# Stores of kept operands on ScalarE's queue, decay gates in the k/b tile, and whole-kilobyte tiles at one address phase

## The chip, the cores and the metric

The kernel runs on one core of a Trainium2 chip. The metric is the device time of one execution in microseconds, the median of several runs; a profiled execution has a time of its own and a span from its first to its last instruction. The core's engines are TensorE (PE, with its weight loads PEld), VectorE (DVE), ScalarE (ACT), GpSimd (POOL) and SyncE (SP). SP computes nothing here: it issues DMAs from its queue, in order.

## The reference, cut to what matters

Two layers, each a mixer, a residual with LayerNorm, a gated feed-forward network and another residual with LayerNorm, over 1024 tokens of 1024 channels. The first mixer is RWKV-7, the second sparse attention (DSA) with an indexer and a top-256 gather.

```python
# layer 0: RWKV-7
xm = x[None] + xx[None] * mix[:, None, None, :]           # six mixed inputs
r, k, v = jnp.einsum('nbsd,nde->nbse', xm[:3], w_rkv)     # three projections
w_log = -jax.nn.softplus(-(w0 + jnp.tanh(xw @ w1) @ w2)) - 0.5
decay = jnp.exp(-jnp.exp(w_log))                          # decay gates
a = jax.nn.sigmoid(a0 + (xa @ a1) @ a2)
...                                                       # scan over tokens, head by head
return y @ w_o
# both layers
def conv_ffn(x, w_up, conv_w, conv_b, w_down):
    u = x @ w_up                                          # 1024 -> 5632
    u = sum(up[:, j:j + S] * conv_w[j] for j in range(CONV_W)) + conv_b
    gate, val = jnp.split(u, 2, axis=-1)
    return (jax.nn.silu(gate) * val) @ w_down             # 2816 -> 1024
```

## The kernel before, in words

**Products.** Nearly every product is made of three matmuls (`mm3`): each operand is split into a high part, rounded to fp32r, and a low part, which is what is left. ACT casts the high part (`split`, L54), POOL or DVE subtracts (L60). L65 is high by high, L66 and L67 have one low part each. A matmul streams the moving operand (512 columns, mostly) while the weights of the next are loaded.

**Stages.** RWKV takes 0 to about 1060 us, the first FFN runs to about 1830 (its up-projections 1130 to 1480, its down-projections after), DSA to about 2480, the second FFN to the end (up-projections 2590 to 2930).

**RWKV.** Tokens come in two halves (hf), channels in two groups (g): four units, (0,0), (0,1), (1,0), (1,1), at roughly 45 to 213, 213 to 460, 460 to 640 and from 640 us. In each unit `lora2` makes the decay gates (sigmoids, L483) and the gate a, `decays` scans the gates along tokens and takes exponentials (L496 to L508), and `proj` makes r, k and v (`pa` in PSUM), each from 8 steps kt of 12 matmuls. A step's operands are a pair of weight tiles (wh, wl) and a pair of mixed inputs (xmh, xml). `pair` (L402 to L416) makes them once and keeps them: they are stored to DRAM (L415, 192 stores of 256 KB), and the unit that needs them again loads them (L409): the inputs when g is 1, the weights when hf is 1. Weights (raw) come by L124. All of these DMAs are issued by SP. Operands, mixed inputs and the four gate tiles `sg` of a unit share the tag of `u`: 14 buffers of 2 KB per partition. `t` has 5 such buffers, AR 2 and BK 1 of 16 KB.

**FFN, up.** Strassen-like products: for each of 22 column blocks f, `up` runs seven products of 12 matmuls (L65 to L67, through `w_mm`). The moving tiles are x11, x21, x22 and the sums xT1 to xT4; the weights are `wo`, split by ACT and POOL from the loaded `wr` or from the sums that DVE makes (S, L884). Results are moved from PSUM (p, pS) into u by ACT (L995 to L1001) or added by DVE (L1004), then the convolution runs (`conv`, ACT L1010, DVE L1015) and the gate (L1023, L1024).

**What sets the order.** A scheduler places each engine's instructions from priorities and costs, and the engines then run their lists in order. Tiles get their addresses from pools that are opened and closed by stage; before the change a pool's tiles follow one another from wherever the pool starts.

Of the kernel before, what the change touches and what calls it, by code (L numbers as in the profile page):

```python
# [17 lines left out]
E05 = math.exp(-0.5)  # L18
# [6 lines left out]
V_MIX, V_W0, V_A0, V_KK, V_KA, V_RK = 0, 48, 56, 64, 72, 80  # L25
# [20 lines left out]
def f32(ap):  # L46
    return ap.bitcast(F32)
# [194 lines left out]
    yield  # L242


class Pools:


# [1 line left out]
        self.tc, self.open = tc, {}  # L249

    def add(self, name, **kw):
        cm = self.tc.tile_pool(name=name, bufs=1, reuse_waits="tile", **kw)
        pool = cm.__enter__()
        self.open[id(pool)] = cm
        return pool

    def psum(self, name, **kw):
        return self.add(name, space=bass.MemoryType.PSUM, **kw)

    def close(self, *pools):  # L260
        for p in pools:
            self.open.pop(id(p)).__exit__(None, None, None)


CFG = {'order': 'k0 r0 a0 A0 v0 x1 l0 l1 x0 d0 b0 i0 w0 W0 r1 d1', 'da': 'p', 'db': 'p', 'kk': 'p', 'uv': 'a', 'go': 'v', 'gz': 'p', 'wr': 'pppv', 'wk': 'vp', 'wv': 'pv', 'xl': 'ppp', 'xp': 'vppppppp', 'p1': 'q0 w q5 i4 t1 at i5', 'n1': 27, 'n2a': 26, 'n2b': 19, 'n3': 20, 'n4': 12, 'qp': 2, 'lag': 2, 'cm': 'pppp', 'phc': 'aaaa', 'olc': 'a', 'qm': 'av', 'quq': 'p', 'quk': 'v', 'sh': 16, 'tc': 'a', 'kve': 'a', 'cB': 'a', 'cU': 'a', 'cY': 'a', 'cV': 'aaaa', 'cR': 'aaaa', 'cT': 'a', 'cM': 'a', 'cUV': 'v', 'sq': 'a', 'kkE': 'a', 'pfl': 'n', 'l2': 'v', 'l1': 'v', 'wo0': 'vppvppvp', 'wl': 'ppvv', 'wl2': 'v', 'wl3': 'vv', 'gz2': 'v', 'yq': 'a', 'pfo': 0, 'pf0': 0, 'pf1': 1, 'pf2': 2, 'dwo0': 'pppppppp', 'dwl': 'vvvv', 'dwl2': 'v', 'dwl3': 'vv', 'tke': 'av', 'rt': 'f2 l0 z f0 f1 p0 p2 l1 f3 p1 p3 p4 l2 l4 l5 l3', 'dt': 'l0 a z l1 p0 p4 p2 p3 p1 l5 l2 l3 l4', 'eT1': 'pvpvvvpv', 'eT3': 'pvpvpppv', 'fs0': 'x0 x1 y1 y0 x2 y2 x3 y3 r0 r1 u0 r3 u3 r2 u4 u6 u2 u7 u5 u1', 'fs1': 'x0 y0 x1 x3 y1 x2 y2 r0 u0 y3 r1 r2 u1 r3 u3 u4 u2 u5 u6 u7', 'eT2': 'vvvvvvvv', 'e22': 'vvvvvvvv', 'eR': 'vvvvvvvv', 'tkp': 'vv', 'kvs': 1, 'ln0': 'pp', 'ln1': 'vv', 'ln2': 'pppppppv', 'ln3': 'pppppppv', 'ln4': ['pp', 'pp'], 'gl': 2, 'ga': '0g1g', 'dl0': 'pppppvppp'}
# [5 lines left out]
def rwkv(k, src, dst):  # L271
    nc, tc = k.nc, k.tc
    E = lambda n: nc.vector if CFG[n] == "v" else nc.gpsimd
    pools = Pools(tc)
    P_, M_ = pools.add("rw", side="left"), pools.add("rwm", side="left")
    PS = pools.psum("rwps")
    DR = k.dram
    zs = Rows(DR, "zs")
# [2 lines left out]
    def u(name, dt=F32):  # L281
        return P_.tile([128, 512], dt, name=name, tag="u", bufs=k.NU)

    def t(name, dt=F32):
        return M_.tile([128, 512], dt, name=name, tag="t", bufs=5)

    def w4(name, shape):
        return P_.tile(shape, F32, name=name, tag="w", bufs=1)

    def acc(name):  # L290
        return PS.tile([128, 512], F32, name=name, tag="acc", bufs=4)
# [18 lines left out]
    smask = M_.tile([128, 512], F32, name="smask")  # L310
# [91 lines left out]
    kept = {}  # L402

    def pair(key, make, again):

        if key in kept:
            hi, lo = u(key[0] + "h", F32R), u(key[0] + "l", F32R)
            for i, x in enumerate((hi, lo)):
                nc.sync.dma_start(f32(x), kept[key][i])  # L409
            return hi, lo  # L410
        hi, lo = make()
        if again:
            kept[key] = DR.tile([2, 128, 512], F32, name="kept_" + "_".join(map(str, key)))
            for i, x in enumerate((hi, lo)):
                nc.sync.dma_start(kept[key][i], f32(x))  # L415
        return hi, lo  # L416

    def operands(hf, n, g, kt):
# [11 lines left out]
    def prefetch(hf, n, g, m):  # L430

        for kt in range(m):
            ahead[hf, n, g, kt] = operands(hf, n, g, kt)
# [23 lines left out]
    def slot(ap, x):  # L457

        return ap.rearrange("p (c x i) -> p c x i", x=2, i=64)[:, :, x, :]

    def v2(ap):
        return ap.rearrange("p (c i) -> p c i", i=64)

    def lora2(hf, g):

        h_ = st[hf]
        AR = P_.tile([128, 4, 1024], F32, name="AR", tag="AR", bufs=2)
        s = un[hf, g] = dict(AR=AR, sg=[])
        if CFG["pfl"] == "b":
            prefetch(hf, 0, g, 1)  # L470
        w2 = wtile(k.w_w2[:, g * 512 : (g + 1) * 512], lo_eng=CFG["l2"])
        a2 = wtile(k.w_a2[:, g * 512 : (g + 1) * 512], lo_eng=CFG["l2"])
        if CFG["pfl"] == "a":
            prefetch(hf, 0, g, 1)
        for i in range(4):
            p = 4 * g + i
            sl = slice(i * 128, (i + 1) * 128)
            s["sg"].append(u("sg"))
            for o, w, h, v0 in ((v2(s["sg"][i]), w2, h_["hw"], V_W0), (slot(AR[:, i], 0), a2, h_["ha"], V_A0)):
                ps = acc("l2")  # L480
                nc.tensor.matmul(ps, w[0][:, sl], h, start=True, stop=False)
                nc.tensor.matmul(ps, w[1][:, sl], h, start=False, stop=True)
                s["last"] = nc.scalar.activation(o, v2(ps), AF.Sigmoid, bias=k.vec[:, v0 + p : v0 + p + 1])  # L483

    def decays(hf, g):
        s = un[hf, g]
        AR, sg = s["AR"], s["sg"]
        BK = P_.tile([128, 4, 1024], F32, name="BK", tag="BK", bufs=1)
        PC = M_.tile([128, 4, 8], F32, name="PC", tag="PC", bufs=2)
        s.update(BK=BK, PC=PC)  # L490
        with tc.issue_after(s["last"].ins):
            for i in range(4):
                p = 4 * g + i
                a_, r_, k_, b_ = slot(AR[:, i], 0), slot(AR[:, i], 1), slot(BK[:, i], 0), slot(BK[:, i], 1)
                c, ip = t("c"), t("ip")
                nc.vector.tensor_tensor_scan(c, smask, sg[i], 0.0, ALU.mult, ALU.add)  # L496
                nc.scalar.activation(ip, c, AF.Exp, scale=E05)
                nc.vector.tensor_tensor(sg[i], c, sg[i], ALU.subtract)
                E("db").tensor_tensor(b_, a_, v2(ip), ALU.mult)
                E("da").tensor_scalar(  # L500
                    a_, a_, k.vec[:, V_KA + p : V_KA + p + 1], omka[:, p : p + 1], ALU.mult, ALU.add
                )
                nc.vector.tensor_tensor(k_, a_, v2(ip), ALU.mult)
                nc.scalar.activation(c, c, AF.Exp, scale=-E05)
                nc.scalar.activation(a_, v2(sg[i]), AF.Exp, scale=-E05)
                nc.gpsimd.tensor_copy(PC[:, i, :], c[:, 63:512:64])
                nc.vector.tensor_tensor(r_, r_, v2(c), ALU.mult)

# [7 lines left out]
    def kproj(hf, g):  # L516
        s = un[hf, g]
        AR, BK = s["AR"], s["BK"]
        a = proj(hf, 1, g, False)
        prefetch(hf, 2, g, PF[2])  # L520
        ss = None
        for i in range(4):
# [4 lines left out]
            else:  # L527
                nc.vector.tensor_scalar(kk, a[i], k.vec[:, V_KK + p : V_KK + p + 1], None, ALU.mult)
            nc.vector.tensor_tensor(slot(BK[:, i], 0), slot(BK[:, i], 0), v2(a[i]), ALU.mult)
            sq = t("sq")  # L530
# [19 lines left out]
        for i in range(4):  # L550
            rb = mi("rb")
            nc.tensor.matmul(rb, selB[:, i, :], rnb, start=True, stop=True)
            nc.vector.tensor_tensor(slot(BK[:, i], 1), slot(BK[:, i], 1), v2(rb), ALU.mult)

# [277 lines left out]
    for j in range(-1, 5):  # L832
        for o in order:
            n, i = o[0], j + int(o[1:])
# [8 lines left out]
    first, last = finish0(Z0), finish1(Z1)  # L843
# [16 lines left out]
def ffn(k, layer, src, dst):  # L860
# [4 lines left out]
    nc, tc = k.nc, k.tc  # L865
    pools = Pools(tc)
    near, far = ("right", "left") if layer == 0 else ("left", "right")
    P_ = pools.add(f"ffp{layer}", side=near)
    L_ = N_ = None
    bufs = {"P": (3, 12), "L": (4, 0), "N": (0, 6)} if layer == 0 else {"P": (2, 12), "L": (5, 0), "N": (0, 7)}  # L870
    hd = [k.dram.tile([2, 128, T], F32, name=f"hd{layer}_{i}") for i in range(NF // 2)]
# [148 lines left out]
    def gated(f):  # L1020
# [4 lines left out]
        nc.sync.dma_start(hd[f // 2][f % 2], val)  # L1025

    psum, k.psum = k.psum, None
    xrs = {}
    w_load(0)
# [10 lines left out]
    for tt in range(4):  # L1040
        if psum:
            run(x_T(tt, lambda: psum("pt")))
        yield
    k.rows = None
    L_, N_ = pools.add(f"ffl{layer}", side=far), pools.add(f"ffn{layer}", side=far)
    PX, PY = pools.psum(f"ffpx{layer}", side="left"), pools.psum(f"ffpy{layer}", side="right")
    if not psum:
        for tt in range(4):
# [19 lines left out]
    half, more, rest = [], [4, 5, 6, 7], [0, 1, 2, 3]  # L1068
    first = [(f, n) for f in range(2) for n in ("11", "12")]
# [147 lines left out]
    for z in range(2):  # L1217
# [4 lines left out]
        i = B_LN + 4 * layer + 2 + z  # L1222
# [4 lines left out]
    for tt in range(8):  # L1227
# [11 lines left out]
        kw = {} if layer else dict(sums=sums, junk=L_.tile([128, 512], BF16, name="lnj", tag="lnj", bufs=1))  # L1239
# [6 lines left out]
def dsa(k, src, dst):  # L1246
    nc, tc = k.nc, k.tc
    TOPK = 256
    NEG = -1e30
    pools = Pools(tc)  # L1250
    P_, T_, PL = pools.add("dsp", side="right"), pools.add("dst", side="right"), pools.psum("dspl", side="right")
    zs = Rows(k.dram, "zd")

    def u(name, dt=F32):
        return P_.tile([128, 512], dt, name=name, tag="u", bufs=6)
# [37 lines left out]
    for h4 in range(2):  # L1293
        uk = u("uk")
        nc.sync.dma_start(uk, k.w_uk[:, 512 * h4 : 512 * h4 + 512])
        for g in range(2):
            gs = slice(64 * g, 64 * g + 64)
            for kt in range(2):
# [6 lines left out]
                o, lo = u("wqk"), u("wqkl", F32R)  # L1305
# [99 lines left out]
    for tt in range(8):  # L1405
# [1 line left out]
        if tt >= LAG:  # L1407
            early(2)
        yield
    M_, PS = pools.add("dsm", side="left"), pools.psum("dsps", side="left")  # L1410
    XTh = M_.tile([128, 4, 1024], F32R, name="XTh")
    XTl = M_.tile([128, 4, 1024], F32R, name="XTl")
    early(len(pend) - 2)
# [538 lines left out]
```

## Time and profile before

| | us |
|---|---|
| median of 3 runs | 3229.09 |
| lowest and highest | 3224.92, 3232.09 |
| profiled execution | 3245.21 |
| its span | 3243.4 |

Over the span PE is busy 2900.3 us (89%), DVE 2471.0 (76%), POOL 1530.5 (47%), ACT 1374.0 (42%). The mean granted clock of TensorE is 0.918 of full speed. A matmul's duration in a row is longer than its distance to the next, since matmuls are pipelined; pace is read from starts. An idle time is put down to the operation that ended it, and waits are given as the waiting engine and line, then who was waited for. SPq is SP's queue: a duration there is that of issuing a DMA, not of the transfer.

### The profile page before, as it was taken

What the parts mean: (1) busy time and instruction counts of PE and PEld (TensorE: products, weight loads), DVE (VectorE), ACT (ScalarE), POOL (GpSimd) and SP (SyncE); (2) the same over time, 40 slices, a digit from 0 to 9 for tenths busy, and PEclk for the clock granted to TensorE, in tenths of its full rate; (3) what the DMA queues carried; (4) which work ended last, traced back from release to release, by engine and by line L of the source; (5) the groups of instructions that cost most, each with busy time, mean ns of one, the idle gap of its engine ahead of it and who ended that gap; (6) DMA issues with size and microseconds to landing.
All of it is one profiled execution on the core that took longest, in us unless ns stands there. A gap on an engine that the chain in (4) does not pass through costs nothing. (4 is left out here: it accounts for less than half of the span.)

```text
span 3243.4 us, 41680 instructions
## 1 busy us (share of the span) xinstructions
PE 2900.3 (89%) x15032; PEld 2260.1 (70%) x15032; DVE 2471.0 (76%) x3925; ACT 1374.0 (42%) x2363; POOL 1530.5 (47%) x987
## 2 busy tenths in 40 slices
PE   7779889989898899999779888888998899999788
PEld 3568657767786677777667766656776677777577
DVE  6684767756757888888876789998475888888975
ACT  3532224322322444444223467776363544444331
POOL 2533105223135666667667612212313666666766
PEclk9878879879798899999889889999999999999899
DMA  5634533535316232235211511102214222235212
GB/s 180 246 131 166 178 101 129 171 118 175 115 56 205 81 89 78 78 91 201 85 65 55 200 56 57 55 33 95 76 48 160 68 78 78 79 98 201 78 52 91
DMA packets 236224, 356.44 MB, mean 110 GB/s; under 512 B 17290, under 2 KB 110858, under 8 KB 235634
## 3 DMA queue, kind: packets, MB, share of 16 engines
q1 hardware_dynamic: 236018, 353.79, 33.2%
q8 instruction: 118, 1.93, 0.2%
q14 instruction: 88, 0.72, 0.1%
HBM read 250.57 MB, written 103.15 MB: 109 GB/s over the span
## 5 line engine op out<-in xcount | busy, mean ns | idle before, releaser
L60 POOL TENSOR_TENSOR wo<-wr,wo 128x512 fp32r<-128x512 f32 x220 | 416.0, 1916 | 282.6 <-ACT wo L54 281.7
L1015 DVE SCALAR_TENSOR_TENSOR cv<-u,vec,cv 128x1023 f32<-128x1023 f32 (+1 forms) x176 | 347.7, 1993 | 53.0 <-ACT cv L1010 51.1
L65 PE MATMUL dn<-dh 128*128 128x512 f32 x532 | 220.8, 415 | 68.5 <-DVE acc L1142 68.3
L60 POOL TENSOR_TENSOR dl<-raw,dh 128x1024 fp32r<-128x1024 f32 x82 | 219.9, 2704 | 102.9 <-ACT dh L54 102.6
L65 PE MATMUL p<-xT,wo 128*128 128x512 f32 x528 | 214.4, 406 | 20.4 <-ACT u L999 11.4
L66 PE MATMUL dn<-dl,dh 128*128 128x512 f32 x532 | 218.2, 410 | 13.0 <-POOL dl L60 6.6
L67 PE MATMUL dn<-dh,dl 128*128 128x512 f32 x532 | 218.2, 410 | 0.0
L1010 ACT ACTIVATE cv<-u,vec 128x1024 f32<-128x1024 f32 x88 | 109.5, 1244 | 254.9 <-DVE u L1004 254.3
L1647 POOL TENSOR_TENSOR cm<-sc,toep 128x256 f32<-128x256 f32 x96 | 75.8, 796 | 293.4 <-DVE mn L1663 225.0
L66 PE MATMUL p<-xT,wo 128*128 128x512 f32 x528 | 210.1, 398 | 3.0 <-DVE xT L60 3.0
L67 PE MATMUL p<-xT,wo 128*128 128x512 f32 x528 | 209.8, 397 | 2.0 <-POOL wo L60 2.0
L1142 DVE SCALAR_TENSOR_TENSOR acc<-acc,dn 128x512 f32<-128x512 f32 x196 | 130.9, 680 | 88.1 <-PE dn L67 88.0
L60 POOL TENSOR_TENSOR wo<-S,wo 128x512 fp32r<-128x512 f32 x88 | 172.7, 1981 | 30.7 <-ACT wo L54 26.4
L54 ACT CAST dh<-raw 128x1024 fp32r<-128x1024 f32 x95 | 94.7, 1046 | 201.2 <-PE dn L67 89.0
L60 POOL TENSOR_TENSOR wl<-wr,wh 128x512 fp32r<-128x512 f32 x56 | 74.8, 1336 | 214.7 <-ACT wh L54 158.1
L65 PEld LDWEIGHTS dn<-dh 128*128 128x128 f32 x532 | 105.7, 199 | 99.1 <-DVE acc L1142 42.0
L65 PE MATMUL pa<-xmh,wh 128*128 128x512 f32 x256 | 114.8, 458 | 48.8 <-ACT xmh L54 24.5
L65 PEld LDWEIGHTS p<-xT,wo 128*128 128x128 f32 x528 | 99.9, 189 | 60.6 <-ACT u L999 27.3
L65 PE MATMUL p<-x,wo 128*128 128x512 f32 x352 | 139.3, 396 | 0.8 <-DVE t L884 0.4
L54 ACT CAST wo<-wr 128x512 fp32r<-128x512 f32 x220 | 127.2, 618 | 28.0 <-POOL wo L60 18.9
L66 PE MATMUL p<-x,wo 128*128 128x512 f32 x352 | 138.7, 394 | 0.0
L67 PE MATMUL p<-x,wo 128*128 128x512 f32 x352 | 138.5, 394 | 0.0
(422 smaller groups left out, 8682.5 us busy)
## 6 DMA issues: line engine op xcount, KB each, us to landing
wr<-in_w_up_dram SPq DMA_DIRECT2D x88, 512.0 KB, 5.9
hd<-cv SPq DMA_DIRECT2D x44, 512.0 KB, 3.4
raw<-hd SPq DMA_DIRECT2D x19, 1024.0 KB, 5.0
raw<-in_w_down_dram SPq DMA_DIRECT2D x19, 1024.0 KB, 7.8
wr<-in_w_wo_dram SPq DMA_DIRECT2D x68, 256.0 KB, 2.9
wr<-in_w_rkv_dram SPq DMA_DIRECT2D x48, 256.0 KB, 3.6
kept_w<-wh SPq DMA_DIRECT2D x48, 256.0 KB, 2.3
kept_w<-wl SPq DMA_DIRECT2D x48, 256.0 KB, 2.1
```

The costliest lines, as they stand in the source:

```text
L54: nc.scalar.copy(hi, raw)
L60: eng.tensor_tensor(lo, raw, f32(hi), ALU.subtract)
L65: mm(ps, lhs[0], rhs[0], start=start, stop=False, **kw)
L66: mm(ps, lhs[0], rhs[1], start=False, stop=False, **kw)
L67: mm(ps, lhs[1], rhs[0], start=False, stop=stop, **kw)
L1010: nc.scalar.activation(o, u, AF.Identity, bias=k.vec[:, cb : cb + 1], scale=k.vec[:, cw[2] : cw[2] + 1])
L1015: nc.vector.scalar_tensor_tensor(o[:, d:], u[:, : 1024 - d], k.vec[:, cw[j] : cw[j] + 1], o[:, d:], ALU.mult, ALU.add)
L1142: nc.vector.scalar_tensor_tensor(o, o, ALPHA if first else 1.0, ps, ALU.mult, ALU.add)
L1647: (nc.vector if CFG["cm"][h4] == "v" else nc.gpsimd).tensor_tensor(cm[:, :near], mk, toep[g][:, h % 8, 256 - near :], ALU.add)
```

## The change

Three parts.

1. `pair` issues the stores of kept operands from ACT (`nc.scalar.dma_start`) rather than from SP. 192 issues leave SP's list (875 rows become 686) and enter ACT's (1560 become 1774).
2. The decay gates are written into the first half of each channel block of BK, the tile that later holds k and b, rather than into four `u` tiles. BK is therefore allocated in `lora2`; in `decays` the difference of scan and gate goes to a new `t` tile d, where it was written in place. k and b then overwrite the gates.
3. `Pools.add` returns an `Even`: two pools, one for tiles whose bytes per partition are a multiple of 1024, one for all others, padded at its end so that the first kind stands at the same address modulo 1024 (992) in every stage.

The cut diff (a line of "..." where something is left out):

```diff
+PHASE = 1024
+SKEW = 576
+class Even:
+    def __init__(self, tc, name, first=False, **kw):
+        self.parts, self.first, self.odd = [], first, {}
+        for n in ("odd", ""):
+            cm = tc.tile_pool(name=name + n, bufs=1, reuse_waits="tile", **kw)
+            self.parts.append((cm, cm.__enter__()))
+    def tile(self, shape, dtype, name, tag=None, bufs=1):
...
+        if n % PHASE == 0 and tag not in self.odd:
+            return self.parts[1][1].tile(shape, dtype, **kw)
+        key = tag or name
+        self.odd[key] = max(self.odd.get(key, 0), -(-n // 32) * 32 * bufs)
+        return self.parts[0][1].tile(shape, dtype, **kw)
+    def close(self):
+        rest = (SKEW * self.first - sum(self.odd.values())) % PHASE
+        if rest:
+            self.parts[0][1].tile([128, rest // 4], F32, name="rest")
...
     def add(self, name, **kw):
-        cm = self.tc.tile_pool(name=name, bufs=1, reuse_waits="tile", **kw)
+        return Even(self.tc, name, **kw)
...
-                nc.sync.dma_start(kept[key][i], f32(x))
+                nc.scalar.dma_start(kept[key][i], f32(x))
...
         AR = P_.tile([128, 4, 1024], F32, name="AR", tag="AR", bufs=2)
-        s = un[hf, g] = dict(AR=AR, sg=[])
+        BK = P_.tile([128, 4, 1024], F32, name="BK", tag="BK", bufs=1)
+        s = un[hf, g] = dict(AR=AR, BK=BK)
...
-            s["sg"].append(u("sg"))
-            for o, w, h, v0 in ((v2(s["sg"][i]), w2, h_["hw"], V_W0), (slot(AR[:, i], 0), a2, h_["ha"], V_A0)):
+            for o, w, h, v0 in ((v2(BK[:, i, :512]), w2, h_["hw"], V_W0), (slot(AR[:, i], 0), a2, h_["ha"], V_A0)):
...
-                c, ip = t("c"), t("ip")
-                nc.vector.tensor_tensor_scan(c, smask, sg[i], 0.0, ALU.mult, ALU.add)
+                c, ip, d = t("c"), t("ip"), t("d")
+                nc.vector.tensor_tensor_scan(c, smask, BK[:, i, :512], 0.0, ALU.mult, ALU.add)
+                nc.vector.tensor_tensor(d, c, BK[:, i, :512], ALU.subtract)
                 nc.scalar.activation(ip, c, AF.Exp, scale=E05)
-                nc.vector.tensor_tensor(sg[i], c, sg[i], ALU.subtract)
...
-                nc.scalar.activation(a_, v2(sg[i]), AF.Exp, scale=-E05)
+                nc.scalar.activation(a_, v2(d), AF.Exp, scale=-E05)
```

`first` is set for the first pool of a side of the memory in each stage, and PSUM's pools stay as they were.

Addresses in bytes per partition, modulo 256, of the tiles that move and of the weights, before. Afterwards all of them stand at 224.

| products | moving tiles | weight tiles |
|---|---|---|
| first FFN, up | x11, x21, xT4: 224; xT1, xT2, xT3, x22: 160 | wo: 224 |
| second FFN, up | x11, x21: 160; xT1 to xT4, x22: 32 | wo: 160 |
| DSA, logits | Q: 224 | XTh, XTl: 160 |

The order of the instructions in DSA and both FFNs is the same on every engine but for the first few of the first FFN.

ACT, the first projection of the first unit (steps kt 0 and 1), before:

```order
L54 CAST wh<-wr 128x512
L351 ACTIVATE xm<-xT,omm 128x512
L54 CAST xmh<-xm 128x512
L351 ACTIVATE xm<-xT,omm 128x512
L54 CAST wh<-wr 128x512
```

And with the change:

```order
L54 CAST wh<-wr 128x512
L387 ACTIVATE xm<-xT,omm 128x512
L451 DMA kept_w_0_0_389<-wh 128x512
L451 DMA kept_w_0_0_389<-wl 128x512
L54 CAST xmh<-xm 128x512
L387 ACTIVATE xm<-xT,omm 128x512
L451 DMA kept_xm_0_0_399<-xmh 128x512
L451 DMA kept_xm_0_0_399<-xml 128x512
L54 CAST wh<-wr 128x512
```

Each cast of a high half now has two stores ahead of it, and the second of them needs the low half of the cast before (wl, xml), which POOL or DVE makes.

SP, the same place, steps kt 2 and 3, before (kept_w_0_2 is the weight of step 2 of projection 0):

```order
L415 DMA kept_xm_0_2_458<-xmh 128x512
L415 DMA kept_xm_0_2_458<-xml 128x512
L124 DMA wr<-in_w_rkv_dram 128x512 x3
L415 DMA kept_w_0_3_479<-wh 128x512
L415 DMA kept_w_0_3_479<-wl 128x512
```

And with the change, from the end of the gate's stores:

```order
L432 DMA gsc<-tg_330 32x512
L124 DMA wr<-in_w_rkv_dram 128x512 x22
L124 DMA wr<-in_w_w_dram 128x512
L124 DMA wr<-in_w_a_dram 128x512
L124 DMA wr<-in_w_rkv_dram 128x512 x3
L445 DMA xmh<-kept_xm_0_0_399 128x512
L445 DMA xml<-kept_xm_0_0_399 128x512
```

The loads of raw weights no longer alternate with stores: 22 stand in a row, and the loads of kept inputs follow without a store between.

## Rows read from the trace of the kernel before

**Rows 1.** Busy us by stretch; last columns: granted clock, DMA share, GB/s.

```profile
45.00:213.00 168.00, 124.71 (x562) 95.41 (x562) 120.05 (x150) 85.18 (x144) 84.28 (x64) 0.83 0.58 206
...
1130.00:1480.00 350.00, 343.35 (x1469) 273.85 (x1468) 302.40 (x215) 160.87 (x244) 240.72 (x124) 1.00 0.30 82
```

**Rows 2.** Timeline of PE in an up-projection: start us, duration us, instruction.

```profile
1239.64 0.39 PE L66 MATMUL p<-x,wo 128*128 128x512 f32 x1
...
1241.91 0.39 PE L67 MATMUL p<-x,wo 128*128 128x512 f32 x1
1242.13 0.39 PE L65 MATMUL p<-xT,wo 128*128 128x512 f32 x1
...
1247.50 0.40 PE L67 MATMUL pS<-xT,wo 128*128 128x512 f32 x1
```

**Rows 3.** Instructions of L66, moving tile x, 1130 to 1470: ns min/median/max.

```profile
L66 PE MATMUL p<-x,wo x136: 389/389/390, 1137.1 to 1461.2; 128*128 128x512 f32 x136
...
L66 PE MATMUL pS<-x,wo x68: 393/394/398, 1131.6 to 1453.0; 128*128 128x512 f32 x68
```

**Rows 4.** Timeline of DVE over one block f, idle time in brackets.

```profile
1234.15 0.69 DVE L1004 TENSOR_TENSOR u<-u,pS 128x512 f32<-128x512 f32 x1 [1.44 <-PE pS L67]
...
1244.66 1.78 DVE L884 TENSOR_TENSOR S<-S,wr 128x512 f32<-128x512 f32 x1
...
1254.11 0.69 DVE L1004 TENSOR_TENSOR u<-u,pS 128x512 f32<-128x512 f32 x1 [1.42 <-PE pS L67]
```

**Rows 5.** Timeline of ACT and PE in the same block.

```profile
1246.53 1.14 ACT L54 CAST wo<-S 128x512 fp32r<-128x512 f32 x2 [3.73 <-DVE S L884]
1247.58 0.58 ACT L999 COPY u<-p 128x512 f32<-128x512 f32 x1
...
1248.21 0.50 PE L65 MATMUL p<-xT,wo 128*128 128x512 f32 x1 [0.31 <-ACT u L999]
```

**Rows 6.** Waits of PE, 1130 to 1480: us, times, longest us.

```profile
PE p L65 <- ACT u L999: 5.6, 17, 0.7
```

**Rows 7.** Waits of PE, 1480 to 1830 (first FFN, down).

```profile
PE dn L65 <- DVE acc L1142: 37.3, 8, 13.2
```

**Rows 8.** Groups on PE, 1830 to 2480 (DSA): busy us, mean ns, idle.

```profile
L65 PE MATMUL lg<-XTh,Q 128*128 128x512 f32 x96 | 43.2, 450 | 9.7 <-DVE mn L1663 7.2 <-DVE Q L60 1.0 <-DVE v L1542 0.9
```

**Rows 9.** Waits of SP's queue, 0 to 700: us, times, longest us.

```profile
SPq L415 <- POOL xml L60: 39.0, 38, 3.5
...
SPq L415 <- POOL wl L60: 33.7, 26, 5.4
...
SPq L409 <- ACT AR L505: 16.5, 4, 12.2
```

**Rows 10.** Instructions by line: issues of L415; low halves on POOL, 45 to 213.

```profile
L415 SPq DMA_DIRECT2D kept_w<-wh x48: 319/327/445, 51.0 to 382.0; - x48
...
L60 POOL TENSOR_TENSOR wl<-wr,wh x16: 1262/1290/1859, 51.1 to 209.2; 128x512 fp32r<-128x512 f32 x16
...
L60 POOL TENSOR_TENSOR xml<-xm,xmh x21: 1267/1548/1742, 54.7 to 179.2; 128x512 fp32r<-128x512 f32 x21
```

**Rows 11.** Waits of ACT, 45 to 213: us, times, longest us.

```profile
ACT B L604 <- PE bps L603: 22.2, 8, 4.5
ACT wh L54 <- DMA wr<-in_w_rkv_dram: 12.7, 3, 7.2
```

**Rows 12.** Timeline of SP's queue around the start of unit (0,1).

```profile
210.63 0.32 SPq L415 DMA_DIRECT2D kept_w<-wl  x1
211.04 0.39 SPq L409 DMA_DIRECT2D xmh<-kept_xm  x1
```

**Rows 13.** Timeline of SP's queue in unit (1,1).

```profile
656.13 0.32 SPq L409 DMA_DIRECT2D xmh<-kept_xm  x1
```

**Rows 14.** Timeline of PE at both places, idle time in brackets.

```profile
213.73 0.77 PE L65 MATMUL pa<-xmh,wh 128*128 128x512 f32 x1 [6.33 <-DMA xmh<-kept_xm]
...
658.70 0.77 PE L65 MATMUL pa<-xmh,wh 128*128 128x512 f32 x1 [9.59 <-DMA xmh<-kept_xm]
```

More of the change, by code (lines that the diff above doesn't have):

```diff
@@ L242, in once @@
     yield
+PHASE = 1024
[7 more added lines that the diff above has]
+    def tile(self, shape, dtype, name, tag=None, bufs=1):
+        n = mybir.dt.size(dtype)
+        for x in shape[1:]:
+            n *= x
+        kw = dict(name=name, tag=tag, bufs=bufs) if tag else dict(name=name)
+        if n % PHASE == 0 and tag not in self.odd:
[7 more added lines that the diff above has]
+            self.parts[0][1].tile([128, rest // 4], F32, name="rest")
+        for cm, _ in reversed(self.parts):
+            cm.__exit__(None, None, None)
 class Pools:
@@ L251, in add, with psum @@
     def add(self, name, **kw):
-        cm = self.tc.tile_pool(name=name, bufs=1, reuse_waits="tile", **kw)
+        return Even(self.tc, name, **kw)
+    def psum(self, name, **kw):
+        cm = self.tc.tile_pool(name=name, bufs=1, reuse_waits="tile", space=bass.MemoryType.PSUM, **kw)
         pool = cm.__enter__()
@@ L255, in add @@
         return pool
-    def psum(self, name, **kw):
-        return self.add(name, space=bass.MemoryType.PSUM, **kw)
     def close(self, *pools):
         for p in pools:
-            self.open.pop(id(p)).__exit__(None, None, None)
+            if isinstance(p, Even):
+                p.close()
+            else:
+                self.open.pop(id(p)).__exit__(None, None, None)
 CFG = {'order': 'k0 r0 a0 A0 v0 x1 l0 l1 x0 d0 b0 i0 w0 W0 r1 d1', 'da': 'p', 'db': 'p', 'kk': 'p', 'uv': 'a', 'go': 'v', 'gz': 'p', 'wr': 'pppv', 'wk': 'vp', 'wv': 'pv', 'xl': 'ppp', 'xp': 'vppppppp', 'p1': 'q0 w q5 i4 t1 at i5', 'n1': 27, 'n2a': 26, 'n2b': 19, 'n3': 20, 'n4': 12, 'qp': 2, 'lag': 2, 'cm': 'pppp', 'phc': 'aaaa', 'olc': 'a', 'qm': 'av', 'quq': 'p', 'quk': 'v', 'sh': 16, 'tc': 'a', 'kve': 'a', 'cB': 'a', 'cU': 'a', 'cY': 'a', 'cV': 'aaaa', 'cR': 'aaaa', 'cT': 'a', 'cM': 'a', 'cUV': 'v', 'sq': 'a', 'kkE': 'a', 'pfl': 'n', 'l2': 'v', 'l1': 'v', 'wo0': 'vppvppvp', 'wl': 'ppvv', 'wl2': 'v', 'wl3': 'vv', 'gz2': 'v', 'yq': 'a', 'pfo': 0, 'pf0': 0, 'pf1': 1, 'pf2': 2, 'dwo0': 'pppppppp', 'dwl': 'vvvv', 'dwl2': 'v', 'dwl3': 'vv', 'tke': 'av', 'rt': 'f2 l0 z f0 f1 p0 p2 l1 f3 p1 p3 p4 l2 l4 l5 l3', 'dt': 'l0 a z l1 p0 p4 p2 p3 p1 l5 l2 l3 l4', 'eT1': 'pvpvvvpv', 'eT3': 'pvpvpppv', 'fs0': 'x0 x1 y1 y0 x2 y2 x3 y3 r0 r1 u0 r3 u3 r2 u4 u6 u2 u7 u5 u1', 'fs1': 'x0 y0 x1 x3 y1 x2 y2 r0 u0 y3 r1 r2 u1 r3 u3 u4 u2 u5 u6 u7', 'eT2': 'vvvvvvvv', 'e22': 'vvvvvvvv', 'eR': 'vvvvvvvv', 'tkp': 'vv', 'kvs': 1, 'ln0': 'pp', 'ln1': 'vv', 'ln2': 'pppppppv', 'ln3': 'pppppppv', 'ln4': ['pp', 'pp'], 'gl': 2, 'ga': '0g1g', 'dl0': 'pppppvppp'}
@@ L274, in rwkv @@
     pools = Pools(tc)
-    P_, M_ = pools.add("rw", side="left"), pools.add("rwm", side="left")
+    P_, M_ = pools.add("rw", first=True, side="left"), pools.add("rwm", side="left")
     PS = pools.psum("rwps")
@@ L486, in decays @@
         s = un[hf, g]
-        AR, sg = s["AR"], s["sg"]
-        BK = P_.tile([128, 4, 1024], F32, name="BK", tag="BK", bufs=1)
+        AR, BK = s["AR"], s["BK"]
         PC = M_.tile([128, 4, 8], F32, name="PC", tag="PC", bufs=2)
-        s.update(BK=BK, PC=PC)
+        s.update(PC=PC)
         with tc.issue_after(s["last"].ins):
@@ L867, in ffn @@
     near, far = ("right", "left") if layer == 0 else ("left", "right")
-    P_ = pools.add(f"ffp{layer}", side=near)
+    P_ = pools.add(f"ffp{layer}", first=layer == 1, side=near)
     L_ = N_ = None
@@ L1044, in ffn @@
     k.rows = None
-    L_, N_ = pools.add(f"ffl{layer}", side=far), pools.add(f"ffn{layer}", side=far)
+    L_, N_ = pools.add(f"ffl{layer}", first=layer == 0, side=far), pools.add(f"ffn{layer}", side=far)
     PX, PY = pools.psum(f"ffpx{layer}", side="left"), pools.psum(f"ffpy{layer}", side="right")
@@ L1409, in dsa @@
         yield
-    M_, PS = pools.add("dsm", side="left"), pools.psum("dsps", side="left")
+    M_, PS = pools.add("dsm", first=True, side="left"), pools.psum("dsps", side="left")
     XTh = M_.tile([128, 4, 1024], F32R, name="XTh")
```

## The prediction

> **What bounds the kernel now.** I read the busy time per stretch first, then the PE timeline of an up-projection, then what PE waits for, and last SP's and ACT's queues in the RWKV layer. In the first FFN's up-projections PE is busy 343.35 of 350 us at a granted clock of 1.00; in the first RWKV projections (45 to 213 us) it is busy 124.71 of 168 us, with ACT busy 85.18 us [rows 1]. So a faster matmul has its best chance in the FFN, and a change of queues only in the RWKV layer.
>
> The pace of matmuls shows what the alignment can touch. In [rows 2] the ten steps from 1239.64 to 1241.91 take 2.27 us, 0.227 us each; the 23 steps from 1242.13 to 1247.50 take 5.37 us, 0.2335 us each. Instruction, shape and clock are the same. What differs is the moving tile: x11/x21, whose address modulo 256 equals that of the weight tiles, against xT and x22, which stand elsewhere (the table of addresses in the section on the change). By tile, p<-x lasts 389 ns at its median, and pS<-x (x22) 394 ns [rows 3]. I read it as 6.5 ns lost where the moving operand and the weights loaded meanwhile have different phases. By the addresses some 4,100 of 9,200 wide matmuls are such before, and about 100 after.
>
> But PE being busy is not PE setting the pace. PE waits 17 times in this stretch for ACT u L999, 5.6 us in all [rows 6]: once per column block f of about 19.95 us. Followed back, that wait is a loop through three engines. DVE waits 1.44 us for PE's pS and starts at 1234.15 [rows 4]; after that neither it nor ACT waits for PE again until S L884 (start 1244.66, 1.78 us). ACT casts S (1246.53) and only then empties the bank (u L999 at 1247.58, 0.58 us) [rows 5]; PE resumes at 1248.21 and reaches the next pS, for which DVE waits 1.42 us until 1254.11 [rows 4]. Of the 19.96 us from 1234.15 to 1254.11, 14.06 us are DVE and ACT work and 5.9 us PE's. **Only the matmuls in those 5.9 us shorten the loop**; the rest turn into a longer wait for u L999.
>
> **Part 3, alignment: the terms.** The 5.9 us hold 24 matmuls, all xT or x22, all of unequal phase: 24 x 6.5 ns = 0.156 us per block. Times 22 blocks and two FFNs (the second has the same order, and its xT and x22 are out of phase too): **-6.8 us**. If PE alone set the pace it would be 48 matmuls per block in the first FFN and 60 in the second, 108 x 22 x 6.5 ns = 15.4 us; that is the other end. In the down-projections some 280 matmuls change phase, 1.8 us, but PE there waits 37.3 us for DVE acc L1142 [rows 7], so I take **-1**. In DSA the logits, scores and absorbed queries hold some 720 wide matmuls and 384 of half width, at most 6 us; the lg matmuls wait 7.2 us for DVE mn L1663 [rows 8], a loop over other engines again, so I take a third, **-2** (0 to -6). In RWKV some 200, mostly at half clock or beside waits: **-0.5**. Nothing in the change shortens DVE, ACT or POOL work. Sum: -10.3 us, between -4 and -23.
>
> The Trainium skill speaks against all of this: "SBUF — State Buffer", section "SBUF: two separate sides", says that on the engine side only the port pair shared by VectorE and GpSimd causes contention, that PE never waits on anyone, and lists a second independent read port for the weight load. By it the alignment is worth nothing, which is rival B. The trace differs as far as it goes: 389 against 394 ns.
>
> **Part 1, stores from ACT.** Removed: 192 issues on SP, which stood in order before the loads. SP's waits for POOL's low halves are 39.0 us (xml) and 33.7 us (wl) [rows 9]: time in which no load behind them goes out. Where PE paid is visible at 213.73: PE sat 6.33 us for xmh from DRAM [rows 14]; SP had the load behind the store of wl, which went at 210.63, and issued it at 211.04 [rows 12]. With the store elsewhere the load can go about 6 us earlier, but this step's wl comes only at 210.6, so PE gains about 3 us, not 6.33. The load one step earlier stands behind such a store in the same way; another 3. ACT waits 12.7 us for weight loads that SP sent late, the longest 7.2 us [rows 11]; in the new order SP sends 22 in a row; PE's part of that I put at a quarter, 3. Gain: **-9**, between 0 and -16.
>
> Added: the same 192 issues on ACT, in order between its casts. The trace of before has no issue on ACT; SP's takes 319 to 445 ns [rows 10], so between 0 and 0.45 us each; I take 0.32, near its median of 327 ns. Worse than the issue is the wait: ACT now stands until the low half exists before it casts the next high half. From 45 to 213 us there are 24 steps and 96 stores. ACT's 85.2 us grow by 96 x 0.32 = 31 to 116. POOL's low halves take 1.29 us (wl) and 1.55 us (xml) [rows 10]; 24 x 2.84 = 68 us, less some 15 for the xm copies that stand between cast and store: 53. That makes 169 of 168 us, before ACT's other waits, such as 22.2 us for PE bps [rows 11]. So **ACT goes from half idle to just full** there. Lower bound 0 (all falls into its 83 idle us), upper bound 169 + 22.2 + 12.7 - 168 = +36. I take a third, **+12**, since PE's own sum in the stretch leaves 43 us and low halves already made PE wait. In the two later units only w or only xm is stored, one wait and two stores per step, and ACT is far from full: **+2** (0 to +8). Queued behind the waits on ACT are the next casts (then POOL, then PE), the evictions of the projections and the copies of the chunk recurrence.
>
> **Part 2, gates in BK.** The four sg tiles no longer take 4 of the 14 u buffers. At 658.70 PE had waited 9.59 us for xmh [rows 14], whose load SP issued only at 656.13 [rows 13], after waiting up to 12.2 us for ACT AR L505 [rows 9], the last reader of sg. That wait has no cause any more. Next late is the decay chain itself, which still ends at the same place on ACT; I take two thirds, **-6** (0 to -10). Allocating BK earlier makes the sigmoids wait for the previous unit's last reader of BK, which in the trace is done before they start: 0. The extra t tile per pass takes 3 of 5 buffers: 0 to +2.
>
> **Sum.** -10.3 - 9 + 12 + 2 - 6 = -11.3 us. The profiled execution took 3245.21 us, 0.5% above the median of the three timed runs (3229.09); I take the difference as absolute: 3234 for such an execution, **3218** for the median.
>
> **Rivals.** A: PE alone sets the pace of the up-projections, so all 15.4 us count. For it: PE's 343.35 of 350 us; against it: the wait for u L999 in nearly every block. 8.6 us more: 3209. B: alignment gives nothing and 389 against 394 ns comes from something else, such as where the moving tiles lie; only RWKV is left, -1: 3228. C, slower: ACT becomes the bound of the first unit and stays late into the second. It decides as soon as waits and issues exceed ACT's 83 idle us, and my sum is 84. At the price of +36 +8 instead of +14 the total is +19: 3248; half of the excess gives 3233. For it: the strict order cast, store, store on ACT; against it: PE already waits there for other things, and freed u buffers let ACT run ahead. D: ACT absorbs the issues and all stalls go (-16, -10): -36 + 2 = -34: 3195. For it: PE's idle time in 45 to 213 us; against it: low halves come when POOL makes them. That the change is not what it says is excluded for order and addresses, which the built kernel shows.
>
> **How the numbers follow.** Forecast 0.44, A 0.12, B 0.10, C 0.16, D 0.18. About 0.2% (6.5 us) is what a measurement of this kernel can tell from no change, so faster means under 3222.6, slower over 3235.5. Faster: 0.33 of the forecast (its own spread is 3206 to 3232), all of D, most of A: 0.62. Same: the rest of the forecast, most of B, the mild end of C: 0.21. Slower: most of C and a little of the forecast and of B: 0.17. The range 3192 to 3234 leaves out the bad half of C and the far end of D.
>
> **What would show it.** Alignment: p<-xT and pS at 389 ns; the up-projection block at 19.8 us, not 19.5 (A) nor 19.95 (B); PE's wait for u L999 above 0.4 us per block. Stores: ACT's waits for POOL wl and xml in 45 to 213 us near 50 us, and that stretch longer by some 10 us; no stall at 213. Gates: no wait of L409's loads for AR, and PE's 9.59 us gone. Wrong I am above all if ACT's issue costs far from 0.32 us, or if PE in the first unit follows ACT step by step.

## The result: slower by 0.9%, and the profile after

The changed kernel took 3262.78 us (median of 4), before 3230.08: a ratio of 1.0093, 95% interval [1.0072, 1.0113]. The two medians alone divide to 1.0101, inside the interval. Measured again later the ratio was 1.0096 [1.0064, 1.0129]. I had forecast 3218 with a range to 3234.

The profiled execution of the changed kernel took 3262.46 us, 17 us more than that of before (3245.21). The latter lies 8 to 15 us above the medians measured for its kernel, so the two traces understate the difference; all verdicts below go by the timed runs, and the traces say where.

**The first unit.** Busy us of PE, PEld, DVE, ACT and POOL from the first projection matmul of unit (0,0) to the first of unit (0,1); then the granted clock. Before, the changed kernel:

```profile
52.20:201.80 149.60, 115.35 (x536) 89.35 (x537) 106.93 (x135) 73.01 (x122) 74.21 (x56) 0.83 0.62 221
```

```profile
53.90:216.50 162.60, 124.61 (x536) 90.66 (x537) 89.89 (x122) 72.10 (x119) 66.00 (x53) 0.83 0.60 209
```

The same 536 matmuls take 13.0 us longer. What ACT does there, from its timeline (start us, duration us; ACTq rows are issues of DMAs):

```profile
62.17 0.62 ACT L54 CAST xmh<-xm 128x512 fp32r<-128x512 f32 x1 [1.19 <-POOL wl L60]
62.69 0.72 ACT L387 ACTIVATE xm<-xT,omm 128x512 f32<-128x512 f32 x1
62.82 0.33 ACTq L451 DMA_DIRECT2D kept_xm<-xmh  x1
64.18 0.33 ACTq L451 DMA_DIRECT2D kept_xm<-xml  x1
64.55 0.62 ACT L54 CAST wh<-wr 128x512 fp32r<-128x512 f32 x1 [1.13 <-POOL xml L60]
...
66.97 0.33 ACTq L451 DMA_DIRECT2D kept_xm<-xmh  x1
68.38 0.33 ACTq L451 DMA_DIRECT2D kept_xm<-xml  x1
68.75 0.62 ACT L54 CAST wh<-wr 128x512 fp32r<-128x512 f32 x1 [1.81 <-POOL xml L60]
```

The store of xmh goes out at 62.82, that of xml only at 64.18, when POOL has made it, and the next cast only then. From one cast of wh to the next (64.55, 68.75) a step takes 4.2 us, in others up to 4.9, where PE needs 2.7 at the pace of 0.227 us per matmul [rows 2]. ACT's waits from 45 to 213 us (us, times, longest) sum it up: 47.1 us in the three rows, 38.5 of them for POOL, where the prediction expected near 50 for POOL. PE's from 45 to 230 us show who pays; before, PE waited 19.1 us for ACT's cast of xmh there, and 14.5 for xmh from DRAM:

```profile
ACT wh L54 <- POOL xml L60: 27.7, 17, 2.8
ACT xmh L54 <- POOL wl L60: 10.8, 8, 1.9
ACT xmh L54 <- DVE wl L60: 8.6, 5, 4.8
```

```profile
PE pa L65 <- ACT xmh L54: 28.9, 13, 14.0
PE pa L66 <- POOL xml L60: 7.2, 12, 2.4
```

The issues themselves are no dearer on ACT (medians of the four groups of stores: 326 to 361 ns) than they were on SP (320 to 379 ns):

```profile
L451 ACTq DMA_DIRECT2D kept_w<-wh x48: 326/326/340, 51.4 to 372.5; - x48
L451 ACTq DMA_DIRECT2D kept_w<-wl x48: 326/361/390, 52.8 to 376.9; - x48
```

**The up-projection.** Instructions of L66 from 1150 to 1490 us in the changed kernel (ns min/median/max), PE's wait from 1130 to 1500, and one block on DVE and PE, which answer to [rows 3 to 6]:

```profile
L66 PE MATMUL pS<-x,wo x68: 389/389/389, 1153.8 to 1473.2; 128*128 128x512 f32 x68
...
L66 PE MATMUL p<-xT,wo x206: 387/389/402, 1151.1 to 1489.4; 128*128 128x512 f32 x103
```

```profile
PE p L65 <- ACT u L1034: 9.5, 18, 0.9
```

```profile
1255.68 0.69 DVE L1039 TENSOR_TENSOR u<-u,pS 128x512 f32<-128x512 f32 x1 [1.31 <-PE pS L67]
...
1266.19 1.78 DVE L919 TENSOR_TENSOR S<-S,wr 128x512 f32<-128x512 f32 x1
...
1275.51 0.69 DVE L1039 TENSOR_TENSOR u<-u,pS 128x512 f32<-128x512 f32 x1 [1.30 <-PE pS L67]
```

```profile
1269.74 0.50 PE L65 MATMUL p<-xT,wo 128*128 128x512 f32 x1 [0.49 <-ACT u L1034]
```

The median matmul of every kind now lasts 389 ns. The block takes 19.83 us (1255.68 to 1275.51) where it took 19.96, and PE waits 0.53 us per block for u, where it waited 0.33.

### The profile page after: what moved, and what is told of

The parts are those of the page before. It is cut to its first block, busy times and chain, and to the rows that moved or that the text cites. A ratio compares the mean times of both kernels' runs of the same rounds, so it can differ in the third digit from the quotient of the medians.

```text
span 3260.6 us, 41650 instructions
## 1 busy us (share of the span) xinstructions
PE 2896.3 (89%) x15032; PEld 2263.2 (69%) x15032; DVE 2459.2 (75%) x3925; ACT 1376.9 (42%) x2363; POOL 1516.8 (47%) x987
## 5 line engine op out<-in xcount | busy, mean ns | idle before, releaser
L65 PE MATMUL p<-xT,wo 128*128 128x512 f32 x528 | 213.3, 404 | 25.4 <-ACT u L1034 19.1
L66 PE MATMUL dn<-dl,dh 128*128 128x512 f32 x532 | 218.4, 411 | 14.4 <-DVE dl L60 7.5
L66 PE MATMUL p<-xT,wo 128*128 128x512 f32 x528 | 208.9, 396 | 3.0 <-DVE xT L60 3.0
L60 POOL TENSOR_TENSOR wl<-wr,wh 128x512 fp32r<-128x512 f32 x56 | 75.1, 1340 | 204.5 <-ACT wh L54 147.9
L54 ACT CAST wh<-wr 128x512 fp32r<-128x512 f32 x108 | 66.6, 621 | 187.2 <-DMA wr<-in_w_w_dram 51.2
L65 PE MATMUL p<-x,wo 128*128 128x512 f32 x352 | 138.8, 394 | 2.1 <-DVE x L60 1.6
L66 PE MATMUL p<-x,wo 128*128 128x512 f32 x352 | 138.1, 392 | 0.0
```

Source lines behind the costliest of these rows:

```text
L54: nc.scalar.copy(hi, raw)
L60: eng.tensor_tensor(lo, raw, f32(hi), ALU.subtract)
L65: mm(ps, lhs[0], rhs[0], start=start, stop=False, **kw)
L66: mm(ps, lhs[0], rhs[1], start=False, stop=False, **kw)
```

## The experiments

All ratios are to before, timed beside it on the same chip, with 95% intervals. Aligned means with part 3. The table has every run but phases, which was run once, for its trace alone.

| kernel | stores | gates | aligned | ratio |
|---|---|---|---|---|
| changed | ACT | BK | yes | 1.0093 [1.0072, 1.0113], again 1.0096 [1.0064, 1.0129] |
| p1_stores | ACT | own | no | 1.0023 [0.9998, 1.0048] |
| p2_gates | SP | BK | no | 1.0023 [1.0003, 1.0043] |
| p3_align | SP | own | yes | 0.9960 [0.9939, 0.9981] |
| p12_stores_gates | ACT | BK | no | 1.0084 [1.0054, 1.0115] |
| p13_stores_align | ACT | own | yes | 1.0007 [0.9980, 1.0033] |
| p23_gates_align | SP | BK | yes | 0.9995 [0.9976, 1.0015] |
| u10_buffers | ACT | BK, u 10 | yes | 1.0088 [1.0061, 1.0114] |
| t6_u13 | ACT | BK, t 6, u 13 | yes | 1.0061 [1.0035, 1.0087] |
| d_in_u | ACT | BK, d in u | yes | 0.9987 [0.9966, 1.0009] |
| bk_claim | ACT | own, BK claimed early | yes | 1.0000 [0.9974, 1.0025] |
| late_stores | ACT, late | BK | yes | 0.9955 [0.9933, 0.9977] |
| late_d_in_u | ACT, late | BK, d in u | yes | 0.9931 [0.9904, 0.9957] |
| late_nogates | ACT, late | own | yes | 0.9910 [0.9881, 0.9939] |
| hi_act | high ACT, low SP | BK | yes | 0.9935 [0.9911, 0.9959] |
| hi_nogates | high ACT, low SP | own | yes | 0.9889 [0.9864, 0.9915] |

### Each part alone

p1_stores is before with `nc.scalar.dma_start` at L415; p2_gates has the changed `lora2` and `decays` alone; p3_align the class `Even` alone; p23_gates_align is the changed kernel with the store line put back:

```diff
-                nc.scalar.dma_start(kept[key][i], f32(x))
+                nc.sync.dma_start(kept[key][i], f32(x))
```

> Part 1 alone: only the stores of kept operands go out from ScalarE's queue; gates and addresses as before. Theory 1 (ScalarE in lock-step: every cast of a high half waits behind the store of the low half before it, 4.8 us for each step of a projection): nearly the whole loss of the changed kernel is here, 1.008 to 1.012 of before (+25 to +38 us), the first stretch of projections longer by 10 to 15 us. Theory 2 (the loss comes from the gates in BK, whose new order delays the decays): within 0.3% of before. Theory 3 (the parts only lose together, because the freed buffers and the store order meet): 1.003 or less here and in the run of the gates alone.

> Part 2 alone: gates in BK and a third t tile, stores from SyncE as before, addresses as before. Theory 1: no loss; the 9.59 us wait for xmh at 658 us goes, but the chunk recurrence behind it is not earlier, so 0.998 to 1.001. Theory 2: 1.006 to 1.010.

> Part 3 alone: whole-kilobyte tiles at one phase modulo 1024; the instructions and their order are those of before. Theory 1 with the loop through DVE and ACT setting the pace of the up-projections: block of 19.84 us against 19.95, some 2.4 us per FFN, with the down-projections about 5 to 8 us in all, 0.9975 to 0.9985. If PE alone set the pace: 0.995. If phases did nothing: 1.000.

> The changed kernel with the one store line put back to SyncE (parts 2 and 3). Theory 1: 0.995 to 0.999, the best of all so far; the difference to the changed kernel, 1.0093, is what the stores cost on ScalarE. Theory 2: 1.004 to 1.008. Theory 3: 0.997 here, with the loss in neither part alone.

Theory 1 fell in half: stores alone cost 0.2%, not 0.8 to 1.2, though their first unit is as long as the changed kernel's (161.6 us against 162.6). Gates alone are not free: 1.0023 lies between the ranges of theories 1 and 2. Alignment gives somewhat more than expected in this one timed pair; by the traces it is 6.0 us outside RWKV (below). The timed pairs with other parts in place (p1 and p13, p2 and p23, p12 and the changed kernel) give -0.16, -0.28 and +0.10%; with this pair's -0.40% the mean is -0.18%, 6 us as well.

### In pairs, and the stores a step later

The pairs are made from the same pieces. In late_stores each pair's stores are issued when two more pairs have been made:

```diff
-            for i, x in enumerate((hi, lo)):
-                nc.scalar.dma_start(kept[key][i], f32(x))
+            late.append((kept[key], (hi, lo)))
+            if len(late) > 2:
+                d, xs = late.pop(0)
+                for i, x in enumerate(xs):
+                    nc.scalar.dma_start(d[i], f32(x))
```

(and the rest at the end of each projection).

> The changed kernel itself, beside the other combinations on one chip. The first measurement gave 1.0093 [1.0072, 1.0113]. Stores alone gave 1.0023, gates alone 1.0023, alignment alone 0.996, gates with alignment 0.9995. If the parts add up, this should be 1.001 to 1.004 and the first measurement was high by the chip or its clock; if they meet, 1.007 to 1.011 again.

> Parts 1 and 2 without the alignment. If stores and gates meet (the four buffers that the gates give up let ScalarE's chain of casts and stores run further ahead and push other work back): 1.010 to 1.014, the changed kernel plus what the alignment gives back (0.4%). If the parts add up: 1.003 to 1.006.

> Parts 1 and 3, gates in their own tiles. If the parts add up, and if stores and gates meet: 0.997 to 1.000. If stores and alignment meet (transfers from the second queue against addresses): 1.006 or more.

> The changed kernel with each pair's stores issued two pairs later on ScalarE, so that a low half has one more step to be made before ScalarE waits for it; the 192 issues stay. If the wait in order is the cost: the first projection shortens from 4.8 us per step to about 4, and the time comes to within 0.3% of gates with alignment (0.998 to 1.003). If the issues themselves are the cost (0.33 to 0.36 us each in the trace of the changed kernel): no better than the changed kernel.

Without alignment, stores and gates give 1.0084 together where 1.0046 would be the sum: between the two expected ranges, and by itself not clear of the sum. With alignment the sum would be 1.0042 (1.0007 + 0.9995 - 0.9960), and the changed kernel gave 1.0093 and 1.0096. Taken together the two comparisons say that stores and gates meet, for some 0.4 to 0.5%. With the stores late, all 192 issues are still ACT's, the first unit takes 143 us, and the time falls below the range expected. **The issues cost nothing that shows; the wait in order for low halves does.** Its window, to be held against the two above:

```profile
52.50:195.50 143.00, 113.03 (x536) 86.50 (x537) 87.66 (x116) 70.35 (x117) 64.52 (x53) 0.86 0.66 235
```

### High halves on ACT, low halves on SP

```diff
-                nc.scalar.dma_start(kept[key][i], f32(x))
+                (nc.scalar, nc.sync)[i].dma_start(kept[key][i], f32(x))
```

> The changed kernel with only the high halves' stores on ScalarE, the low halves' back on SyncE. ScalarE then waits only for its own casts; 96 of the 192 issues stay on it. If the wait for low halves is the cost: the first unit takes 143 to 148 us rather than 163, and the time is 0.998 to 1.002. If it is the order of casts and stores that the scheduler makes: 1.006 or more.

> Aligned tiles, gates in their own tiles, high halves stored from ScalarE and low halves from SyncE. If waiting for low halves is what hurts on ScalarE, and the third temporary is what the gates cost: 0.987 to 0.992, below the same with gates (0.9935). If low halves on SyncE bring back the blocked loads: 0.993 to 0.997.

0.9935 with gates in BK and 0.9889 without, the fastest of all. In hi_act no store on ACT waits for a low half, the first unit takes 142.1 us, and the time lies below both ranges expected. SP's waits from 45 to 213 us in hi_act:

```profile
SPq L451 <- POOL xml L60: 42.0, 13, 12.7
SPq L451 <- POOL wl L60: 31.3, 17, 6.5
```

In the same window before has:

```profile
SPq L415 <- POOL wl L60: 16.3, 16, 5.4
SPq L415 <- POOL xml L60: 14.0, 19, 1.4
```

SP thus waits for low halves more than ever, and the kernel is faster all the same, though PE waits 6.4 us for xml from DRAM from 45 to 230 us, which before does not show. What moving the high halves takes from SP is another wait, that before shows from 0 to 700 us:

```profile
SPq L415 <- ACT wh L54: 118.5, 34, 13.0
SPq L415 <- ACT xmh L54: 96.4, 23, 18.5
```

These are stores that stood on SP until ACT came to the cast. On ACT the cast stands ahead of its store in the same list. That these waits are what held the loads fits all of this, but is argued: no run leaves the high halves on SP and moves the low halves alone.

### What the gates cost

u10_buffers sets `k.NU` from 14 to 10. t6_u13 gives tag t 6 buffers and u 13. d_in_u and bk_claim split part 2:

```diff
-                c, ip, d = t("c"), t("ip"), t("d")
+                c, ip, d = t("c"), t("ip"), u("d")
```

```diff
+            nc.scalar.copy(BK[:, i, :1], s["sg"][i][:, :1])
```

(the second with BK allocated in `lora2` and the gates in their own tiles).

> The changed kernel with 10 buffers of operands rather than 14, which is what the gates left of them before. If stores and gates meet because the four freed buffers let the chain of casts and stores run further ahead: 1.000 to 1.004, as stores with alignment (1.0007). If the gates' own order is the cause (third temporary, BK claimed earlier): 1.008 or more.

> The changed kernel with 6 temporaries of tag t rather than 5 and 13 operand buffers rather than 14. If the third temporary of a decay pass is what makes gates and stores lose together (mixed inputs wait for a buffer of t): 1.002 to 1.006. If not: 1.008 to 1.011 as the changed kernel.

> The changed kernel with the decay difference d in an operand buffer (tag u) rather than in a third temporary (tag t). If the third temporary is what the gates cost (mixed inputs, squares and exponentials wait for one of 5 buffers): 1.000 to 1.004, near stores with alignment (1.0007). If the early claim of BK is the cost: 1.007 to 1.011, as the changed kernel.

> Stores on ScalarE and alignment, gates in their own tiles, and one element of each gate copied into BK, so that BK is claimed where the changed kernel claims it. If the early claim of BK is the cost of the gates: 1.007 to 1.011. If the third temporary is: 1.000 to 1.003.

Claiming BK early is not it (1.0000). With d in an operand buffer the loss is gone (0.9987); with one more t and one u less it is probably smaller (1.0061, the intervals overlap). **Beside stores in order, d in tag t is what the gates cost.** The freed operand buffers are not closed as a rival: with 10 buffers the ratio stays (1.0088), but the trace loses the time in another place (the tables below), and d_in_u takes operand buffers for d, so that it also leaves fewer free. The direct waits for d are small; on DVE, from 45 to 700 us in the changed kernel:

```profile
DVE d L532 <- POOL xml L60: 3.7, 1, 3.7
...
DVE d L532 <- ACT AR L540: 0.8, 1, 0.8
```

> Aligned tiles, stores on ScalarE two pairs late, gates in BK with the decay difference in an operand buffer. If the third temporary is all that the gates cost: at least as fast as the same without gates (0.991 [0.988, 0.994]), and faster by up to 0.3% if the gates do save the wait for xmh. If gates in BK cost something else too: 0.994 to 0.997, as late stores with gates (0.9955).

With the stores late, d in u gives 0.9931 and d in t 0.9955; the intervals overlap. For late_nogates, 0.990 to 0.994 was expected if the gates cost by themselves, and 0.994 to 0.997 if they cost only beside stores in order. It gave 0.9910: by themselves. Two other pairs agree. With d in t and no store in order, the gates cost 0.45% here, 0.46% in hi_act against hi_nogates and 0.35% in p23_gates_align against p3_align, 11 to 15 us. With d in u the two pairs (d_in_u against p13_stores_align, late_d_in_u against late_nogates) give -0.20 and +0.21%, which cannot be told from nothing. In no aligned pair did the gates in BK bring a gain that is clear of noise. Why is open.

### The phases

phases is p3_align with the five moving tiles of the second FFN's far side allocated 64 bytes apart from the common phase:

```diff
+            z = pool.parts[1][1].tile([128, 4096 + 16], dt, name=name, tag="big", bufs=bufs["L"][0])[:, :4096]
```

> Alignment alone, but in the second FFN the five moving tiles of the far side stand off the weights by 192 (xT2), 256 (xT4), 320 (xT3), 384 (x22) and 448 (xT1) bytes. If the phase modulo 256 decides: xT4 at 389 ns per matmul, the other four at 393 to 398. If modulo 512 or 1024 decides: all five at 393 to 398. If it is a matter of 64-byte lines: all at 389.

From the starts of PE's rows at a granted clock of 1.00, by tile; offset of the moving tile from the weights:

| tile | offset modulo 512 | ns from start to start, mean | median duration |
|---|---|---|---|
| x11, x21 | 0 | 226.7 | 389 |
| xT4 | 256 | 231.0 | 393 |
| xT3 | 320 | 229.6 | 392 |
| x22 | 384 | 233.0 | 393 |
| xT1, xT2 | 448, 192 | 233.3 | 394 |

An offset of 256 is not as good as none, so "modulo 256" in the prediction is wrong; equal modulo 512 is the loosest condition that ran at 226.7 ns here: the four weight slices of a product stand 512 bytes apart, and matmuls on all four ran at that pace. The row of xT3 says little, since this product follows PE's wait for u and takes 229.1 ns in the mean in p3_align too, where it is aligned.

## Why the prediction was wrong, point by point

**The up-projections: right, a little too large.** The loop through DVE and ACT set the pace, as worked out (but for 0.26 us that ACT does wait for PE, at 1236.89): 0.125 us per median block against 0.156 forecast, 5.5 us for 44 blocks against 6.8. The 12 xT3 matmuls of the loop account for the difference: they went from 233.2 to 229.2 ns, not to 226.7. PE's wait for u grew in exchange, which closes rival A (PE alone, 15.4 us). Rival B is closed as well: the pace of matmuls follows the phase, 226.7 against up to 233.3 ns. The Trainium skill ("SBUF — State Buffer", section "SBUF: two separate sides") says that PE never waits on anyone. Read as the prediction read it, that the alignment is worth nothing, this does not agree with these paces, and the measurement decides.

**Down-projections and DSA.** Averages over the traces of the four kernels without alignment and of 14 with it: first FFN's up-projections 454.1 and 451.9 us, its down-projections 300.7 and 299.5, DSA 698.5 and 698.2, the second FFN 721.5 and 719.1. So the down-projections gave 1.2 us (forecast 1) and DSA nothing that shows (forecast 2); that its loops over other engines [rows 8] are the reason was not tested. The up-projections gave 2.2 us in the first FFN by this measure, somewhat less than 22 median blocks. In all it is -6.0 outside RWKV against -9.8 forecast.

**The cost of the stores: right in place and mechanism, too small.** I put +12 us on the first unit, and the unit is 13.0 longer, by the mechanism named: ACT waiting for each low half. But the 13.0 are net of what the freed SP gives there. Against the same stores two pairs later the first unit is 19.6 us longer (162.6 and 143.0), and over the kernel p13_stores_align against late_nogates makes the wait in order 0.97%, about 31 us (give or take 13) where I had 14. That 12 and 13.0 agree so well is in part luck.

**The gain of the stores: wrong in its reading.** I gave -9 for loads no longer stuck behind stores, and argued from SP's waits for low halves [rows 9]. hi_act leaves those waits on SP and is fast. What most likely held the loads were the stores of high halves, 118.5 and 96.4 us of waiting for casts, which I had not costed. The gain is also larger: late_nogates is 0.50% below p3_align, some 16 us (give or take 12), hi_nogates 0.71%, some 23. Cost and gain were both too small, so that for part 1 alone my +5 us came near the 0.23% (7 us) of p1_stores. The stall at 213.73 [rows 14] did go; what came next is this, in the changed kernel:

```profile
226.66 1.17 PE L65 MATMUL pa<-xmh,wh 128*128 128x512 f32 x4 [1.32 <-DMA xmh<-kept_xm]
231.89 0.80 PE L67 MATMUL pa<-xmh,wl 128*128 128x512 f32 x1 [3.54 <-DVE wl L60]
```

PE now waits for the low half of the weight, as the prediction said, so that half the stall stays.

**The gates: the step that failed worst.** The 9.59 us wait for xmh [rows 14] is gone, as forecast; PE's waits from 640 to 720 us in the changed kernel begin with:

```profile
PE xps L678 <- DVE TX L666: 8.1, 1, 8.1
```

In before this wait was 3.4 us. p2_gates shows the same exchange (8.3 us), and p1_stores does not (9.5 us for xmh, 3.0 for TX), so it is the gates'. The projection no longer waits for xmh, and the chunk recurrence behind it waits instead: the unit (1,1) takes 218.2 us after and 215.4 before. So -6 became 0 at this place. And "the extra t tile, 0 to +2 us" was mis-sized by a factor of ten or more: d_in_u is about 1% faster than the changed kernel on the same work. Together I had the gates at -6 to -4 us; they cost 11 to 15 by themselves and, beside stores in order, some 28 (the changed kernel against p13_stores_align). The sum had no term for parts that meet. I had looked for a wait for BK and found none, rightly (bk_claim), and had given five buffers that many names share one sentence.

**The sum.** Of -11.3, RWKV was to give -1; it lost some 37 (31 by the ratio 1.0096, and the 6 that alignment gave elsewhere), and either edit alone takes all or most of that loss away: the stores two pairs later (late_stores, 0.9955) or d out of tag t (d_in_u, 0.9987), where alignment alone is at 0.9960. Rival C had the right sign and place, the order cast, store, store on ACT. Its price was not right: with it, stores alone would have cost some 35 us (44 less the 9 gained), and p1_stores cost 7. The loss needed the gates too.

**What is left open.** How a third temporary that shows 4.5 us of direct waits on DVE costs some 35 us. The places, first: us from the first projection matmul of each unit to that of the next, for (1,1) to the output projection, and from there to the first `p` of the FFN.

| kernel | (0,0) | (0,1) | (1,0) | (1,1) | rest |
|---|---|---|---|---|---|
| before | 149.6 | 244.8 | 196.5 | 215.4 | 204.1 |
| changed | 162.7 | 240.8 | 206.5 | 218.2 | 202.6 |
| changed, again | 163.4 | 241.6 | 199.1 | 217.9 | 202.2 |
| p13_stores_align | 162.6 | 239.9 | 194.5 | 220.0 | 196.2 |
| d_in_u | 159.2 | 221.8 | 196.2 | 212.4 | 204.5 |
| u10_buffers | 165.5 | 238.1 | 192.8 | 235.1 | 193.3 |

Beside the first unit, (1,0) is the one that is longer where stores in order meet d in t: the two rows of the changed kernel, and 210.6 us in p12_stores_gates and 208.9 in t6_u13, against 196.0 in p1_stores and 188.8 in bk_claim. With 10 buffers (1,0) is short and (1,1) long: the same ratio, another loss.

Part of the answer is the granted clock. From the first matmul to the first `p` of the FFN I took from each of 19 traces the duration, the time at which the granted clock was half, and PE's idle time:

| kernel | duration us | half clock us | PE idle us | duration - half/2 - idle |
|---|---|---|---|---|
| before | 1056.6 | 326.7 | 125.6 | 768 |
| p3_align (same instructions) | 1044.6 | 289.4 | 129.3 | 771 |
| changed, two executions | 1078.4, 1068.9 | 341.5, 327.4 | 137.4, 136.8 | 770, 768 |
| p12_stores_gates | 1075.1 | 333.4 | 139.5 | 769 |
| u10_buffers | 1070.1 | 266.7 | 159.1 | 778 |
| d_in_u | 1040.1 | 255.0 | 133.9 | 779 |
| bk_claim | 1037.5 | 253.4 | 133.8 | 777 |
| late_nogates | 1024.1 | 256.9 | 127.5 | 768 |
| hi_nogates | 1010.7 | 230.7 | 119.9 | 775 |

The last column stays within 767 to 779 in all 19, while durations go from 1011 to 1078. So of the changed kernel's loss against p3_align one part is PE's idle time (+8 us) and another, larger one is time at 1.2 GHz (half of +52 and +38 us), and d_in_u differs from the changed kernel in the second, hardly in the first. u10_buffers loses by idle time instead. Half-clock time varies between executions of one instruction list (289 to 327 us in before, p3_align and phases), so a single trace does not prove this; what in the order of work raises it was not singled out.

## What to carry to other kernels

Issue a DMA from the engine that has just produced the bytes: here that cost 0.33 us each and no wait (hi_act). Put on an engine that must wait for another's result, it stopped everything behind it in that engine's list, some 31 us in all; issue it a step later or elsewhere. A new temporary in a tight shared pool can change the order of much else: here it cost some 35 us beside stores in order, with 4.5 us of direct waits, so do not price one by its direct waits.

## What the runs showed of the hardware that I had not expected

A matmul of 512 columns at a granted clock of 1.00 follows the one before by 226.7 ns where moving operand and weights have equal addresses modulo 512, and by up to 233.3 ns where not (phases); in the up-projections of before and p3_align no median duration of DVE's or ACT's operations differs by more than 5 ns. The issue of a DMA takes 326 to 361 ns on ACT, by medians, and 320 to 379 on SP.
